# Block products from the first pair on in the second feed-forward of a one-layer encoder step

## The chip, the cores and the metric

The kernel runs on one core of a Trainium2 chip. The metric is the device time of one execution, in microseconds, as the median of several runs. Beside the times there is the trace of one profiled execution, which gives each engine's instructions with their start and length. The engines are TensorE (matmuls; PE in the rows, and PEld for its weight loads), VectorE (DVE), ScalarE (ACT), GpSimd (POOL, which issues the accumulating DMAs) and SyncE (SP, which issues the weight loads).

## The reference

One layer of a streaming encoder over 512 prompt rows and 64 sample rows, 576 in all, width 1024:

```python
x = x + 0.5 * swiglu_ffn(rms_norm(x, ffn1_norm), ffn1_w_gate_up, ffn1_w_down)
h = rms_norm(x, mix_norm); p = h @ w_in        # gated convolutions, merged and multiplied by w_out
...
x = x + merged @ w_out
x = x + 0.5 * swiglu_ffn(rms_norm(x, ffn2_norm), ffn2_w_gate_up, ffn2_w_down)
y = rms_norm(x, final_norm)

def swiglu_ffn(x, w_gate_up, w_down):          # hidden width 2816
    gate, up = jnp.split(x @ w_gate_up, 2, axis=-1)
    return (jax.nn.silu(gate) * up) @ w_down
```

The inputs are float32, and the kernel keeps nearly that precision.

## The kernel before, in words

Activations lie with the feature on the 128 partitions and the 576 rows along the free axis, so x is eight tiles X[0..7] of 128x576. A product of float32 values is made of three matmuls in a shorter type: each operand is split into a high part (rounded) and a low part (the value less its high part), and high x high, high x low and low x high are added in PSUM. A matmul takes 128 features by 288 rows, one half of the rows.

**Plain and block form.** The hidden columns of a feed-forward are worked off in 22 tiles of 128, each with a gate and an up weight; a tile with both is called a pair here. In the plain form (`plain`, line 750) gate and up are two products of 8 feature tiles x 2 halves x 3 matmuls, 96 in all. In the block form (`pair`, line 787) the 2x2 problem of (gate, up) by (first 512 features, last 512 features) and the two halves of the rows is done with seven products in place of eight, in Strassen's way: 7 x 4 feature tiles x 3 matmuls, 84 in all. Its weights are a11, a12 (gate), a21, a22 (up) and four sums s1 to s4 of them; its right operands are parts of the scaled rows themselves for three of the products (a11, a12 and s4), and for four products the "forms" t1 to t4, sums and differences of quarters of the rows, which class `Forms` (line 572) makes: `scale` on ScalarE, `combine` with four VectorE operations and two roundings on ScalarE, `split` with the two low parts on VectorE. `PLAIN` (line 52) says how many pairs are plain: four in the first feed-forward, one in the second.

**Weights.** Class `Stream` (line 195) brings all weights in the order of use, in units of up to 512 features x 128 columns. A raw weight is loaded by an SP queue DMA. `add` makes a weight sum on VectorE, `begin` rounds the unit's high part on ScalarE, and the low part comes in one of two ways. With "dve", VectorE subtracts the high part (`end`). With "dma", ScalarE also writes the negated high part and a POOL DMA adds the raw value onto it. `lead` (line 287) does these ahead of use: when TensorE's code gets unit n, units up to n + 5 are ended, up to n + 7 added and up to n + 6 begun. A unit's two parts live in a pair of tiles of the pool "u" or of another pool, in turn.

**Order.** The calls of each engine are kept in the order of the Python program (class `Ordered`, line 71), so an operation waits for all that the program puts on its engine before it, also where that waits for another engine.

**Around the change.** The products with w_out (loop at line 1132) run j in the order 0, 4, 1, 5, 2, 6, 3, 7. After each, VectorE adds it to X[j], `split_scaled` makes the high (ScalarE) and low part (VectorE) of the row tile times its norm gain, ScalarE squares X[j] for the norm's sum, and the forms are begun. After the loop `gather` adds up the squares and splits the sum, and the last forms are made. Then the second feed-forward begins with plain pair 0, whose gate product takes the feature tiles in the same order, so that X[7] comes last. Between its gate and its up product four matmuls total the squares over the partitions, and `rstd` (line 556) takes the reciprocal root R on VectorE and ScalarE; the gate is multiplied by R before SiLU. Block results stand in one PSUM bank each, eight in all (`bank`, line 157).

Of the kernel before, what the change touches and what calls it, by code (L numbers as in the profile page):

```python
# [13 lines left out]
P = 128  # L14
D = 1024
KT = D // P
# [4 lines left out]
KU = KT // 2  # L21
# [27 lines left out]
WARM = 10  # L49


PLAIN = {"f1": 4, "f2": 1}

IN_TURN = (0, 4, 1, 5, 2, 6, 3, 7)

# [51 lines left out]
def tile_encoder_step(  # L107
# [38 lines left out]
    def wtile(dt=F32, n=LB - HB):  # L146
        return conv.tile([P, LB - HB], dt, tag="w", name=nm("w"), bufs=6)[:, :n]

    def ttile(dt=F32):
        return tmp.tile([P, T], dt, tag="tmp", name=nm("tmp"))  # L150
# [40 lines left out]
    def par(j, r, n=1):  # L191
        return gains[:, r : r + n, j] if r < R_CA else prm[:, r - R_CA : r - R_CA + n, j]
# [115 lines left out]
    def home(other):  # L308

        homes[0] += 1  # L310
        return ("u", other)[homes[0] % 2]
# [13 lines left out]
    def plan_pair(f, gu, i):  # L325

        plan_block((f, "s", i), [
            ws.raw(gu, h * KU * P, KU, gu_col(part, i)) for part in "ug" for h in range(2)  # L330
        ], [home("g") for _ in range(7)], "dve" if (f, i) == ("f1", PLAIN[f]) else "dma")

    def plan_block(name, raws, homes, low="dma"):

        a21, a22, a11, a12 = raws
        s1, s2, s3, s4 = ((name, n) for n in range(1, 5))
        plan[name] = [
            ws.unit(src, KU, home, how, sums)
            for home, (src, how, sums) in zip(homes, (
                (a11, low, ((s1, (a21, a22)),)),  # L340
                (s2, "dve", ((s2, (s1, a11)),)),
                (s1, "dve", ()),
                (s3, "dve", ((s3, (a11, a21)),)),
                (a12, low, ()),
                (s4, "dve", ((s4, (s2, a12)),)),
                (a22, low, ()),
            ))
        ]

    def plan_ffn(f, gu, dn):  # L350
# [24 lines left out]
    def plan_mixer(name, w, col):  # L375
        plan_tile(name, w, 0, (KU, KU), col, "act")
# [12 lines left out]
    for j in range(KT):  # L389
        plan_mixer(("yb", j), w_b_out, j * P)  # L390
    for j in IN_TURN:
        plan_mixer(("o", j), w_out, j * P)
    plan_ffn("f2", ffn2_gu, ffn2_dn)


# [13 lines left out]
    def chunks(name):  # L409

        got = []
        for n in plan[name]:
            w = ws.get(n)
            got += [(w, kk) for kk in range(ws.units[n][1])]
        return got

    def block(w, xs):

        q = bank()[:, :H]
        for k in range(KU):  # L420
            (whi, wlo), (xh, xl) = w, xs[k]
            for m, (l, r) in enumerate(((whi, xh), (whi, xl), (wlo, xh))):
                pe.matmul(q, l[:, k, :], r, start=k == m == 0, stop=k == KU - 1 and m == 2)
        return q
# [19 lines left out]
    def product(name, xs, then=None, order=None, got=None):  # L444

        if name in early:
            return early.pop(name)[:, :, :H]
        ps = psum2()
        if order or got:
            got = got or chunks(name)  # L450
            for n, k in enumerate(order or range(len(xs))):
                mm(ps, *got[k], xs[k], n == 0, n == len(xs) - 1)
        else:
            k = 0
            for n in plan[name]:
                w = ws.get(n)
                for kk in range(ws.units[n][1]):
                    mm(ps, w, kk, xs[k], k == 0, k == len(xs) - 1)
                    k += 1
        take()  # L460
        if then is None:
            dve.time = max(dve.time, pe.time)
            return ps[:, :, :H]
        fill()
        behind.append((pe.time, lambda: then(ps[:, :, :H])))
# [106 lines left out]
    class Forms:  # L572
# [3 lines left out]
        def __init__(self, r_g):  # L576
            self.r_g, self.b, self.t, self.parts = r_g, {}, {}, {}

        def scale(self, p):
            self.b[p] = [wtile(n=T) for _ in range(2)]  # L580
            for b, j in zip(self.b[p], (p, p + KU)):
                sca.activation(b, X[j], AF.Copy, scale=par(j, self.r_g))

        def combine(self, p):
            (b1, b2), (c, d) = self.b.pop(p), (ttile() for _ in range(2))
# [157 lines left out]

    def ffn(f, xg, sums, finish, forms, R=None, todo=()):
        todo = list(todo)

        rest = []


        def plain(i, hs):  # L750
            nonlocal R
            t, up = ttile(), (f, "u", i)
            ps = product((f, "g", i), xg, order=IN_TURN if f == "f2" and i == 0 else None)
            got = None if up in early else chunks(up)
            if R is None:
                R = rstd(sums)
            ups = product(up, xg, got=got)
            hs.append(None)
            at = len(hs) - 1

            def gate():
                dve.tensor_tensor(halves(t), ps, halves(R), op=ALU.mult)
                sca.activation(t, t, AF.Silu)

            def hidden():
                dve.tensor_tensor(halves(t), ups, halves(t), op=ALU.mult)
                hs[at] = high(t)

            def parts():
                hs[at] = hs[at], low(t, hs[at])  # L770

            if f == "f2":
                rest.extend((gate, hidden, parts))
                return
            gate()
            forming()
            hidden()
            forming()
            parts()
            forming()  # L780

        def forming():
            if todo:
                for step, p in todo.pop(0):
                    step(p)

        def pair(i, hs, last):
            qu, uu, t, cu = (ttile() for _ in range(4))
            q1, u2, u3, u4 = half(qu, 0), half(qu, 1), half(uu, 0), half(uu, 1)
            q = []  # L790

            def q7():
                dve.tensor_tensor(u3, q[3], u2, op=ALU.add)
                dve.tensor_tensor(half(cu, 1), u3, q[2], op=ALU.subtract)

            def gate():
                dve.tensor_tensor(half(t, 1), q[5], u4, op=ALU.add)
                dve.tensor_tensor(t, t, R, op=ALU.mult)
                sca.activation(t, t, AF.Silu)

            steps = (
                lambda: sca.copy(q1, q[0]),
                lambda: dve.tensor_tensor(u2, q[1], q1, op=ALU.subtract),
                lambda: dve.tensor_tensor(u4, q[2], u2, op=ALU.subtract),
                q7,
                lambda: dve.tensor_tensor(half(t, 0), q[4], q1, op=ALU.add),
                gate,
            )
            for n, xs in enumerate(bs):
                q.append(block(ws.get(plan[f, "s", i][n]), xs))  # L810
                if n > 0:
                    steps[n - 1]()
                if rest:
                    rest.pop(0)()

            hs.append(None)
            at = len(hs) - 1

            def up():
                if last:  # L820
                    dve.tensor_tensor(t, t, R, op=ALU.mult)
                dve.tensor_tensor(half(cu, 0), q[6], u3, op=ALU.add)

            def hidden():
                dve.tensor_tensor(cu, cu, t, op=ALU.mult)
                hs[at] = high(cu)

            def parts():
                hs[at] = hs[at], low(cu, hs[at])

            rest.extend((up, hidden, parts))

        for g, grp in enumerate(GROUPS):
            hs = []
            for i in grp:
                if i < PLAIN[f]:
                    plain(i, hs)
                    continue
                if i == PLAIN[f]:
                    ws.ahead = AHEAD_UNITS  # L840
                    bs = forms.operands(xg)
                pair(i, hs, grp[-1] == FT - 1)
            while rest:
                rest.pop(0)()
            spare.clear()
            if grp[-1] < FT - 1:
                for j, ps in enumerate(both([(f, "d", g, j) for j in range(2)], hs)):
                    update(j, ps, R)
                for j in range(2, KT):
                    update(j, product((f, "d", g, j), hs), R)  # L850
            else:
                finish(g, hs)
# [279 lines left out]
    for n, j in enumerate(IN_TURN):  # L1132
        ps = product(("o", j), MS)
        dve.tensor_tensor(halves(X[j]), ps, halves(X[j]), op=ALU.add)
        xg[j] = split_scaled(X[j], par(j, R_N2))
        ss.square(X[j])
        ss.add(dve)
        p = n // 2
        if n % 2:
            forms.scale(p)  # L1140
        elif p > 0:
            forms.combine(p - 1)
            if p > 1:
                forms.split(p - 2)
    ss.gather()
    forms.combine(KU - 1)
    forms.split(KU - 2)
    forms.split(KU - 1)


    def finish2(g, hs):
# [112 lines left out]
```

## Time and profile before

| | us |
|---|---|
| median of 3 runs | 1298.48 |
| lowest, highest | 1298.05, 1299.4 |
| the profiled execution's own time | 1297.62 |
| its span, first to last instruction | 1295.8 |

The span is what the rows below are timed in; 1.82 us of the profiled execution lie outside it. TensorE's busy share says little by itself, since matmuls overlap; what counts is whether one group of matmuls starts when the former one's spacing ends. The row of a group gives its start, its length, the engine, the operation, out<-in by names, shapes, the count and, in brackets, the idle time before it with what ended it.

### The profile page before, as it was taken

The page shows a single profiled execution, that of the slowest core. Times are in us where ns is not written, and L with a number is a line of the kernel's source. Part 1 is how long each engine was busy: PE and PEld are TensorE (multiplying, and loading weights), DVE is VectorE, ACT ScalarE, POOL GpSimd, SP SyncE. Part 2 cuts the span into 40 slices and gives each one's busy share as a digit, 9 for nine tenths or more (in the row PEclk, how much of TensorE's full clock was granted, in tenths as well). Part 3 has the DMA queues.
Part 4 walks back from the last instruction along what each step waited for, and adds up shares of the span by engine and source line. Part 5 has one row for each costly group of instructions (what it writes and reads, how often), then busy time and mean ns, then how long its engine had stood idle before and what let it go on. Part 6 is the DMA issues. An engine that isn't in the chain of part 4 may idle for free.

```text
span 1295.8 us, 25664 instructions
## 1 busy us (share of the span) xinstructions
PE 1283.5 (99%) x9754; PEld 1281.9 (99%) x9754; DVE 897.0 (69%) x1480; ACT 763.7 (59%) x1351; POOL 372.0 (29%) x470
## 2 busy tenths in 40 slices
PE   9999999999999999999999999999999999999996
PEld 9999999999999999999999999999999999999996
DVE  6868668648846998898884160336867858847955
ACT  7655646546776655555544674467665656654664
POOL 0032332232333444333321322222242242241230
PEclk9999999999999999999999999999999999999998
DMA  7286786886798898877885977776697696796782
GB/s 215 74 180 153 164 179 153 175 181 151 151 194 185 168 206 175 169 168 169 178 170 117 211 158 164 169 154 139 145 179 171 145 199 149 161 206 140 159 176 80
DMA packets 285931, 213.15 MB, mean 164 GB/s; under 512 B 15344, under 2 KB 248816, under 8 KB 285808
## 3 DMA queue, kind: packets, MB, share of 16 engines
q0 software_dynamic: 57600, 95.05, 44.9%
q1 hardware_dynamic: 226336, 115.49, 31.4%
q8 instruction: 77, 1.26, 0.4%
q10 hardware_dynamic: 1872, 0.97, 0.3%
q14 instruction: 46, 0.38, 0.1%
HBM read 113.81 MB, written 2.62 MB: 90 GB/s over the span
## 4 chain that ended last, share of the span: by engine, by line
PE 96%; DVE 2%; ACT 1%; DMA 1%; issue 0%; DVEq 0%; SPq 0%; ACTq 0%
PE mm L83 96%; DVE acc L83 0%; DMA raw<-in_ffn_w_gate_up_dram 0%; ACT tmp L83 0%; DVE tmp L83 0%; DVE g L83 0%; DVE act L83 0%; DMA gains<-in_params_dram 0%; ACT act L83 0%; DVE x L83 0%; ACT g L83 0%; DVEq L1254 0%; DVE r L83 0%; ACT r L83 0%; ACT acc L83 0%
## 5 line engine op out<-in xcount | busy, mean ns | idle before, releaser
L83 PE MATMUL mm<-act,u 128*128 128x288 f32 x4686 | 659.8, 293 | 0.0
L83 PEld LDWEIGHTS mm<-act,u 128*128 128x128 f32 x4686 | 630.5, 188 | 0.0
L83 PE MATMUL mm<-act,g 128*128 128x288 f32 x2778 | 398.8, 294 | 0.1
L83 PEld LDWEIGHTS mm<-act,g 128*128 128x128 f32 x2778 | 377.5, 188 | 0.3 <-DVE tmp L83 0.3
L83 PE MATMUL mm<-act,act 128*128 128x288 f32 (+2 forms) x2244 | 306.1, 293 | 0.0
L83 PEld LDWEIGHTS mm<-act,act 128*128 128x128 f32 x2244 | 297.3, 188 | 0.0
L83 POOL DMA_DIRECT2D u<-raw x197 | 172.5, 876 | 409.9 <-ACT u L83 298.2
L83 ACT CAST u<-raw 128x512 fp32r<-128x512 f32 (+2 forms) x203 | 116.2, 572 | 156.1 <-PE mm L83 119.1
L83 POOL DMA_DIRECT2D g<-raw x117 | 102.3, 874 | 272.9 <-ACT g L83 212.7
L83 DVE SCALAR_TENSOR_TENSOR w<-g,prm,w 128x606 f32<-128x606 f32 x232 | 179.2, 842 | 1.4 <-ACT w L83 1.4
L83 DVE TENSOR_TENSOR tmp<-mm,tmp 128x288 f32<-128x288 f32 (+1 forms) x239 | 107.6, 458 | 67.8 <-PE mm L83 50.9
L83 POOL DMA_DIRECT2D act<-raw x86 | 74.7, 869 | 196.1 <-ACT act L83 187.7
L83 ACT ACTIVATE u<-u 128x512 fp32r<-128x512 f32 (+2 forms) x197 | 116.9, 593 | 6.2
L83 ACT CAST g<-raw 128x512 fp32r<-128x512 f32 (+2 forms) x126 | 69.0, 548 | 39.1 <-DMA raw<-in_ffn_w_down_dram 15.8
L83 DVE SCALAR_TENSOR_TENSOR tmp<-mm,r 128x576 f32<-128x576 f32 x48 | 36.3, 757 | 71.8 <-PE mm L83 71.8
L83 ACT CAST u<-w 128x512 fp32r<-128x512 f32 x79 | 48.9, 619 | 60.1 <-DVE w L83 52.8
L83 ACT CAST g<-w 128x512 fp32r<-128x512 f32 x77 | 47.7, 619 | 60.1 <-DVE w L83 51.5
L83 ACT CAST act<-tmp 128x576 fp32r<-128x576 f32 x84 | 56.7, 675 | 42.7 <-DVE tmp L83 41.1
L83 DVE TENSOR_TENSOR act<-tmp,act 128x576 fp32r<-128x576 f32 x84 | 62.1, 755 | 18.2 <-ACT act L83 16.5
L83 ACT ACTIVATE g<-g 128x512 fp32r<-128x512 f32 (+2 forms) x117 | 66.4, 568 | 3.7
L83 ACT CAST act<-raw 128x512 fp32r<-128x512 f32 (+3 forms) x94 | 55.6, 592 | 14.5 <-PE mm L83 6.6
L83 DVE TENSOR_TENSOR w<-raw,raw 128x512 f32<-128x512 f32 x78 | 53.4, 685 | 12.8 <-DMA raw<-in_ffn_w_gate_up_dram 12.8
(88 smaller groups left out, 808.6 us busy)
## 6 DMA issues: line engine op xcount, KB each, us to landing
raw<-in_ffn_w_gate_up_dram SPq DMA_DIRECT2D x171, 256.0 KB, 3.4
u<-raw POOLq DMA_DIRECT2D x140, 256.0 KB, 4.1
raw<-in_w_in_dram SPq DMA_DIRECT2D x112, 256.0 KB, 3.6
act<-raw POOLq DMA_DIRECT2D x80, 256.0 KB, 4.0
raw<-in_ffn_w_down_dram SPq DMA_DIRECT2D x96, 192.0 KB, 3.8
g<-raw POOLq DMA_DIRECT2D x60, 256.0 KB, 3.9
g<-raw POOLq DMA_DIRECT2D x43, 192.0 KB, 4.5
u<-raw POOLq DMA_DIRECT2D x41, 192.0 KB, 4.5
```

Source lines behind the costliest of these rows:

```text
L83: return self.tc.keep_in_program_order(fn(*args, **kwargs))
```

## The change

In the second feed-forward pair 0 is done in block form as well (`PLAIN["f2"]` is 0). It runs its seven products in another order, `FORMS_LAST`: a11, a12 and s4, whose right operands are the rows themselves, come first, then the four that need forms. The sums are made in the order that this asks for, its s3 only just before its unit. The sum over squares is totalled, and R taken, after the sixth product, and pair 0's gate is put off into pair 1. For pairs 0 and 1 the low parts of the sums s1 to s4 are made by ScalarE and a POOL DMA in place of VectorE. In the loop over w_out, one scaled copy for the forms follows each X[j], ahead of its square, where two followed every second one behind it; the forms' low parts come earlier; and the gathering of the squares comes behind the last forms and not ahead of them. The weights of these products live in "u" and "g" (the pool of the convolution) in turn, and not in "u" and "act".

```diff
-PLAIN = {"f1": 4, "f2": 1}
+PLAIN = {"f1": 4, "f2": 0}
+
+FORMS_LAST = (0, 4, 5, 1, 2, 3, 6)
...
+            "dma" if f == "f2" and i < 2 else "dve", order_of(f, i))
+
+    def order_of(f, i):
+        return FORMS_LAST if (f, i) == ("f2", 0) else range(7)
+
+    def plan_block(name, raws, homes, low="dma", low_s="dve", order=range(7)):
         a21, a22, a11, a12 = raws
         s1, s2, s3, s4 = ((name, n) for n in range(1, 5))
+        units = (
+            (a11, low), (s2, low_s), (s1, low_s), (s3, low_s), (a12, low), (s4, low_s), (a22, low)
+        )
+        at = (0, 4, 3, 5) if order == FORMS_LAST else (0, 1, 3, 5)
+        sums = dict(zip(at, (
+            (s1, (a21, a22)), (s2, (s1, a11)), (s3, (a11, a21)), (s4, (s2, a12))
+        )))
...
     for j in IN_TURN:
-        plan_mixer(("o", j), w_out, j * P)
+        plan_tile(("o", j), w_out, 0, (KU, KU), j * P, "g")
...
+            order = order_of(f, i)
+            late = ()
+            if order == FORMS_LAST:
+                steps[5], late = (lambda: None), (gate,)
+            q = [None] * 7
+            for m, n in enumerate(order):
+                q[n] = block(ws.get(plan[f, "s", i][m]), bs[n])
+                if R is None and m == 5:
+                    R = rstd(sums)
+                if m > 0:
+                    steps[order[m - 1]]()
                 if rest:
                     rest.pop(0)()
...
-            rest.extend((up, hidden, parts))
+            rest.extend((*late, up, hidden, parts))
...
         xg[j] = split_scaled(X[j], par(j, R_N2))
+        p = n // 2
+        forms.scale(p, (j,))
         ss.square(X[j])
-        ss.add(dve)
-        p = n // 2
-        if n % 2:
-            forms.scale(p)
-        elif p > 0:
+        if n < KT - 1:
+            ss.add(dve)
+        if n % 2 == 0 and p > 0:
             forms.combine(p - 1)
-            if p > 1:
-                forms.split(p - 2)
+        if n in (3, 5, 6):
+            forms.split((n - 2) // 2)
+
+    forms.combine(KU - 1)
+    forms.split(KU - 1)
+    ss.add(dve)
     ss.gather()
-    forms.combine(KU - 1)
-    forms.split(KU - 2)
-    forms.split(KU - 1)
```

## Rows read from the trace of the kernel before

**Rows 1.** The page: busy time of the engines, and the chain's shares.

```profile
PE 1283.5 (99%) x9754; PEld 1281.9 (99%) x9754; DVE 897.0 (69%) x1480; ACT 763.7 (59%) x1351; POOL 372.0 (29%) x470
...
PE 96%; DVE 2%; ACT 1%; DMA 1%; issue 0%; DVEq 0%; SPq 0%; ACTq 0%
```

**Rows 2.** Timeline of TensorE, 897 to 922 us: start, length, engine, operation, count.

```profile
897.66 0.94 PE L83 MATMUL mm<-act,g 128*128 128x288 f32 x6
...
903.90 0.69 PE L83 MATMUL mm<-tmp,ones_r 128*128 128x288 f32 x4
...
910.75 1.74 PE L83 MATMUL mm<-act,g 128*128 128x288 f32 x12
...
921.87 1.74 PE L83 MATMUL mm<-act,u 128*128 128x288 f32 x12
```

**Rows 3.** Stretches: length, busy PE, PEld, DVE, ACT, POOL; clock, DMA share, GB/s.

```profile
1282.00:1286.00 4.00, 2.33 (x16) 1.69 (x14) 3.01 (x7) 2.23 (x6) 0.00 (x0) 1.00 0.69 234
897.60:908.70 11.10, 11.10 (x87) 11.10 (x86) 9.23 (x17) 6.48 (x11) 0.86 (x1) 1.00 0.30 71
```

**Rows 4.** Timeline of ScalarE, 888 to 927 us.

```profile
888.05 1.43 ACT L83 ACTIVATE w<-x,gains 128x576 f32<-128x576 f32 x2
...
892.41 0.78 ACT L83 ACTIVATE act<-x,gains 128x576 fp32r<-128x576 f32 x1 [0.58 <-DVE x L83]
893.09 0.67 ACT L83 ACTIVATE tmp<-x 128x576 f32<-128x576 f32 x1
...
901.54 0.66 ACT L83 CAST tmp<-acc 128x576 fp32r<-128x576 f32 x1
903.95 1.41 ACT L83 CAST act<-tmp 128x576 fp32r<-128x576 f32 x2 [1.74 <-DVE tmp L83]
905.26 0.62 ACT L83 CAST g<-w 128x512 fp32r<-128x512 f32 x1
...
911.22 0.69 ACT L83 ACTIVATE r<-tmp 128x576 f32<-128x576 f32 x1
...
925.48 0.69 ACT L83 ACTIVATE tmp<-tmp 128x576 f32<-128x576 f32 x1 [0.85 <-DVE tmp L83]
926.08 0.60 ACT L83 CAST u<-raw 128x512 fp32r<-128x512 f32 x1
926.71 0.63 ACT L83 ACTIVATE u<-u 128x512 fp32r<-128x512 f32 x1
```

**Rows 5.** Timeline of VectorE, 893 to 926 us.

```profile
893.22 0.82 DVE L83 SCALAR_TENSOR_TENSOR act<-x,gains,act 128x576 fp32r<-128x576 f32 x1 [0.85 <-ACT act L83]
893.96 0.75 DVE L83 TENSOR_TENSOR acc<-acc,tmp 128x576 f32<-128x576 f32 x1
894.63 0.45 DVE L83 TENSOR_TENSOR tmp<-w 128x288 f32<-128x288 f32 x1
...
896.23 1.42 DVE L83 TENSOR_TENSOR act<-tmp,act 128x576 fp32r<-128x576 f32 x2
897.56 0.68 DVE L83 TENSOR_TENSOR w<-w,raw 128x512 f32<-128x512 f32 x1
...
913.52 0.76 DVE L83 SCALAR_TENSOR_TENSOR r<-tmp,r 128x576 f32<-128x576 f32 x1
...
923.84 0.81 DVE L83 TENSOR_TENSOR tmp<-mm,tmp 128x288 f32<-128x288 f32 x2
924.69 0.76 DVE L83 TENSOR_TENSOR tmp<-tmp,r 128x576 f32<-128x576 f32 x1
```

**Rows 6.** Timeline of POOL, 927 to 929 us.

```profile
927.63 0.86 POOL L83 DMA_DIRECT2D u<-raw  x1 [3.69 <-DVE w L83]
```

**Rows 7.** DMA issues at 892.1, 913.4 and 918.3 us: count, KB, us to landing.

```profile
u<-raw POOLq DMA_DIRECT2D x1, 256.0 KB, 6.0
...
g<-raw POOLq DMA_DIRECT2D x1, 256.0 KB, 3.7
...
u<-raw POOLq DMA_DIRECT2D x1, 256.0 KB, 3.2
```

More of the change, by code (lines that the diff above doesn't have):

```diff
@@ L330, in plan_pair @@
             ws.raw(gu, h * KU * P, KU, gu_col(part, i)) for part in "ug" for h in range(2)
-        ], [home("g") for _ in range(7)], "dve" if (f, i) == ("f1", PLAIN[f]) else "dma")
-    def plan_block(name, raws, homes, low="dma"):
+        ], [home("g") for _ in range(7)], "dve" if (f, i) == ("f1", PLAIN[f]) else "dma",
+            "dma" if f == "f2" and i < 2 else "dve", order_of(f, i))
+    def order_of(f, i):
+        return FORMS_LAST if (f, i) == ("f2", 0) else range(7)
+    def plan_block(name, raws, homes, low="dma", low_s="dve", order=range(7)):
         a21, a22, a11, a12 = raws
         s1, s2, s3, s4 = ((name, n) for n in range(1, 5))
-        plan[name] = [
[L338 to L347, printed above, removed]
+        units = (
[5 more added lines that the diff above has]
+        )))
+        plan[name] = [
+            ws.unit(units[n][0], KU, home, units[n][1], (sums[n],) if n in sums else ())
+            for n, home in zip(order, homes)
         ]
@@ L577, in __init__, with scale @@
             self.r_g, self.b, self.t, self.parts = r_g, {}, {}, {}
-        def scale(self, p):
-            self.b[p] = [wtile(n=T) for _ in range(2)]
-            for b, j in zip(self.b[p], (p, p + KU)):
+        def scale(self, p, js=None):
+            for j in js or (p, p + KU):
+                b = wtile(n=T)
                 sca.activation(b, X[j], AF.Copy, scale=par(j, self.r_g))
+                self.b.setdefault(p, []).append(b)
         def combine(self, p):
@@ L750, in plain @@
         def plain(i, hs):
-            nonlocal R
             t, up = ttile(), (f, "u", i)
[L753 to L757, printed above, removed]
+            ps = product((f, "g", i), xg)
+            ups = product(up, xg)
             hs.append(None)
@@ L770, in parts @@
                 hs[at] = hs[at], low(t, hs[at])
-            if f == "f2":
-                rest.extend((gate, hidden, parts))
-                return
             gate()
@@ L787, in pair @@
         def pair(i, hs, last):
+            nonlocal R
             qu, uu, t, cu = (ttile() for _ in range(4))
             q1, u2, u3, u4 = half(qu, 0), half(qu, 1), half(uu, 0), half(uu, 1)
-            q = []
             def q7():
@@ L799, in gate @@
                 sca.activation(t, t, AF.Silu)
-            steps = (
+            steps = [
                 lambda: sca.copy(q1, q[0]),
@@ L807, in pair @@
                 gate,
[L808 to L812, printed above, removed]
+            ]
+            order = order_of(f, i)
[9 more added lines that the diff above has]
+                    steps[order[m - 1]]()
                 if rest:
```

## The prediction

> **What bounds the kernel now.** I read the page first: TensorE is busy for 99% of the span, and the chain that ended last is TensorE for 96% of it [rows 1]. So an edit pays only by what it does to the train of matmuls: fewer of them, or a gap in it. Then I read the timeline of TensorE around the start of the second feed-forward [rows 2]. Pair 0, in plain form, starts at 897.66, its 48 gate matmuls end at 903.90 (6.24 us, 0.130 each), four matmuls of the row sums follow (0.52), and pair 1, the first in block form, starts at 910.75. The reader is to see that one group begins where the former one's spacing ends: TensorE never waits here. Third, the table of stretches [rows 3]: in pair 0's 11.1 us the other engines have room (ScalarE 6.48, the DMA engines 0.30 of their time). Last, the timelines of ScalarE and VectorE, for the order in which each works off its queue; that order decides this case.
>
> **The gain.** A plain pair is 2 x 8 x 6 = 96 matmuls, a block pair 7 x 12 = 84. Plain pair 0 takes 910.75 - 897.66 - 0.52 = 12.57 us; pair 1 in blocks takes 921.87 - 910.75 = 11.12, or 1.59 a block [rows 2]. The change turns one pair from the one into the other: 12.57 - 11.12 = 1.45 us saved if TensorE still never waits. Nothing else is taken off TensorE.
>
> **What moves onto the queues.** The low parts of eight weight sums (four in each of pairs 0 and 1) leave VectorE: per sum one 128x512 subtraction, about 0.68 like the addition at 897.56 [rows 5], gives way to a multiplication on ScalarE, 0.63, and a POOL DMA that lands 3.2 to 3.7 us after its issue [rows 4, 6, 7]. VectorE has no use for the relief, since it didn't hold TensorE; ScalarE gets 8 x 0.63 = 5 us more, within 22 us. Both engines keep the program's order. The trace shows it: the next weight's rounding at 905.26 comes only after the last forms' rounding, issued at 903.95 [rows 4], though its data lay ready.
>
> I number the weight units in the order of use: 0 to 6 pair 0, 7 to 13 pair 1, 14 the first of pair 2. The stream starts unit n + 6 when it gets unit n, so units 0 to 5 are queued before the last output product's own work, and unit 6 only after that product's scaling, the last forms and the gathering of the row sums. Before the change that was harmless: pair 1's units had 12.57 us of plain matmuls ahead of them. Now block 6 is wanted 6 x 1.59 + 0.52 = 10.1 us after the start.
>
> **ScalarE's and VectorE's path, step by step,** from the next to last output product, whose scaled row is there as before, at 892.41 + 0.78 [rows 4]:
> - The new order puts one scaled copy (half of 1.43) before the square that took 893.09 to 893.76. The addition to the row sums starts 0.5 late, at 894.5 in place of 893.96, and the four combinations (1.60 from the first to what follows) end near 896.8 [rows 4, 5].
> - The forms' second rounding (half of 1.41) 897.5, its low part (half of 1.42) 898.25, and sum s3, which now stands here (0.68), 898.9.
> - ScalarE's rounding and negation of s3 (0.60 + 0.63) end at 900.15, and only then comes the last row's scaled rounding (0.78), 900.95; VectorE's low part of it (0.82) ends at 901.8.
> **First wait:** the second block, a12, reaches that row in its fourth quarter at 897.66 + 1.59 + 10 x 0.13 = 900.55. It waits 1.25 us.
> - The last forms: combinations 1.60, 903.4; rounding 0.70, 904.1; low part 0.71, 904.8. Forms-using blocks start after 903.7 and want the last row later still: no wait.
> - Gathering: addition 0.75, 905.55; rounding 0.66, 906.2 [rows 4, 5].
> - Unit 6, rounding and negation: 907.4. POOL issues 0.3 after the negation (927.63 against 926.71 + 0.63), at 907.7 [rows 4, 6]; landing after 3.45 us, the middle of rows 7's 3.2 and 3.7: 911.2.
> **Second wait:** without any wait block 6 would want these low parts in its third matmul, at 897.66 + 10.06 + 0.26 = 907.98. They are 3.2 us late, the first wait included.
> - Units 6 to 11 go through ScalarE at 1.17 each (1.23 less the overlap of 0.06), with one 128x288 copy between them, about 0.3: from 906.2 to 913.5. The root of the row sums stands behind them. In the trace, from ScalarE's part at 911.22 to VectorE's last at 913.52 + 0.76 is 3.06 [rows 4, 5]; here 916.6. Before it was done at 914.28.
> - Four short VectorE operations at 0.40 (two took 0.81), one weight sum at 0.6, the product with the root 0.76: 919.6. SiLU (0.69) 920.3. Behind SiLU on ScalarE stands unit 14: 1.23, 921.5; POOL 921.8; landing 925.3 [rows 4 to 7].
> **Third wait:** without waits block 14 would want it at 897.66 + 14 x 1.59 + 0.52 + 0.26 = 920.7. It is 4.6 us late, the first two waits included, since TensorE cannot pass block 6 or block 14.
>
> **Sum:** -1.45 + 4.6 = +3.15, say +3.2 us. Later units have time again: from pair 2 on only three lows in seven are DMAs, and the gate returns to its own pair.
>
> **The other edits,** at nothing. Output weights in the conv pool in place of the activations': the convolution's tiles there are free long before; if one weren't, a unit would begin a block late, 0 to 1.6 us, and with six units ahead I take 0. A later release of the second gate bank: TensorE's tenth block wants a bank at about 917 to 918, when VectorE is at the release; 0 to 1 us, inside the third wait. Weight loads on SP keep their number. TensorE's clock: the waits are 1.25, 2 and 1.4 us, in separate places; in 1282 to 1286 TensorE was busy 2.33 of 4.00 us and the clock was still 1.00 [rows 3], so I charge nothing.
>
> **The landing time** is the term least sure. Rows 7 show 3.2 and 3.7 where the engines were little used, and 6.0 for a low part that ran with another and a weight load (issued at 892.1). The Trainium skill says in "DMA: Bandwidth & Descriptors", Issuing engines are not separate DMA queues, that DMAs of all issuers run on the same 16 engines and interleave. That speaks against this change, which adds eight to a stretch with loads; the 6.0 agrees with it. By the quiet rows the sum is +3.2; with 6.0 at unit 14 it is +3.2 + 2.5 = +5.7. I take the quiet rows, as VectorE and ScalarE space the last of these issues apart; the ends of this term are +2.9 (3.2) and +5.7.
>
> **Rivals.**
> 1. The queues keep up and only the matmuls count: -1.45 us, 1297.0, faster by less than can be told, not slower. For it: the stretch has much idle ScalarE and DMA time [rows 3]. Against it: the order of the queue, not its load. It decides if unit 6's negation is through by 904.2 (907.98 - 3.45 - 0.3) and unit 14's by 916.9.
> 2. Only block 6 waits, and the SiLU comes early enough to hide unit 14: -1.45 + 3.2 = +1.75, 1300.2, no change that can be told. It decides if the root's ScalarE part runs by 912.1 (913.5 less the 1.4 between 4.6 and 3.2), before the last weights of pair 1 and not behind them. The code says behind.
> 3. DMAs pile up: eight lows within ten us, with loads between them, land at 6.0 in place of 3.45: +5.7, 1304.2. For it: rows 7's 6.0. Against: DMA engines idle for 0.70 of pair 0 before [rows 3].
> 4. A gain above the count: VectorE's relief closes gaps in TensorE's train. There are none in rows 2, so under 5%.
>
> **How the numbers follow.** The profiled execution took 1297.62 us, 1.82 beside its span of 1295.8; the median of three is 1298.48. The sum is made against the profile and carried to the median: 1298.48 + 3.2 = 1301.7. Changes under 0.2% (2.6 us) can't be told from none. Chances: forecast 0.50 (its own range 1300.5 to 1303.5; 0.06 of it under 2.6), rival 3 0.14, rival 2 0.19, rival 1 0.13, rival 4 0.04. Slower: 0.44 + 0.14 = 0.58. Same: 0.06 + 0.19 + 0.13 = 0.38. Faster: 0.04. The range 1297.6 to 1304.4 reaches to rival 3 and past rival 2, and leaves out most of rival 1.
>
> **What would show it.** After: pair 0 in seven groups of 12 matmuls; TensorE waiting for VectorE's or ScalarE's scaled last row some 2.7 us after the feed-forward's start, then for POOL's DMA at block 6, then at pair 2's first block, which stands 3 us later than 921.87 against the start at 897.66. The root's ScalarE part is behind six units' weights. If pair 2's first block starts at 920.4, rival 1 is right; if block 6 waits and pair 2 doesn't, rival 2. The forecast is wrong if either engine passed these operations in another order, or if waits outside this stretch appear.

## The result, and the profile after

The changed kernel takes 1303.38 us (median of 6 runs, 1303.11 to 1304.84) against 1298.37 (6 runs, 1297.96 to 1299.4) in the same runs: ratio 1.0042, interval 1.0032 to 1.0052, so it is slower by 4.2 to 6.8 us. The prediction said 1301.7, in 1297.6 to 1304.4, and slower with a chance of 0.58. The profiled execution took 1304.21 us, with a span of 1302.4.

On the page of the profile after, TensorE's busy share stays at 99%, while its share of the chain falls from 96% [rows 1] to 82%:

```profile
PE 1285.6 (99%) x9742; PEld 1281.9 (98%) x9742; DVE 901.1 (69%) x1487; ACT 769.5 (59%) x1362; POOL 377.1 (29%) x477
...
PE 82%; issue 10%; DMA 2%; DVE 2%; ACT 2%; POOL 2%; POOLq 0%; DVEq 0%; ACTq 0%; SPq 0%
```

The timeline of TensorE after, from the start of the second feed-forward (start, length, engine, operation, count, idle time before it with what ended it), answers to [rows 2], which had no wait at all:

```profile
898.03 1.74 PE L85 MATMUL mm<-act,g 128*128 128x288 f32 x12
...
901.50 0.40 PE L85 MATMUL mm<-act,u 128*128 128x288 f32 x1 [0.55 <-ACT act L85]
902.36 0.54 PE L85 MATMUL mm<-act,u 128*128 128x288 f32 x2 [0.46 <-DVE act L85]
...
910.09 0.53 PE L85 MATMUL mm<-act,g 128*128 128x288 f32 x2 [0.31 <-DVE tmp L85]
911.76 1.60 PE L85 MATMUL mm<-act,g 128*128 128x288 f32 x10 [1.15 <-DMA g<-raw]
...
913.94 1.58 PE L85 MATMUL mm<-act,u 128*128 128x288 f32 x10 [0.31 <-DMA u<-raw]
...
916.19 1.60 PE L85 MATMUL mm<-act,g 128*128 128x288 f32 x10 [0.41 <-DMA g<-w]
...
920.73 1.58 PE L85 MATMUL mm<-act,g 128*128 128x288 f32 x10 [0.85 <-DMA g<-w]
...
927.95 1.59 PE L85 MATMUL mm<-act,g 128*128 128x288 f32 x10 [0.41 <-DMA g<-raw]
...
938.91 1.74 PE L85 MATMUL mm<-act,u 128*128 128x288 f32 x12
...
1253.51 3.65 PE L85 MATMUL mm<-act,g 128*128 128x288 f32 x26 [0.71 <-DMA g<-raw]
```

How to read it: after a block that waits for nothing the next one starts 1.59 us later. What a block takes beyond that is its loss. It is more than the idle time in brackets, by some 0.16 to 0.37 us for each wait; what makes up the rest is not shown. From the starts of all blocks (not all shown): block 1 (a12, the last row) loses 1.53; block 6 loses 0.47 for its PSUM bank, then 1.52 for its low part; blocks 7 to 11 lose 0.57, 0.68, 0.24, 1.10 and 0.17; block 14 loses 0.67. The sum is 6.95. Less the 1.45 that the matmul count saves, that is 5.5, and so it stands: pair 3 starts 938.91 - 898.03 = 40.88 after pair 0, where it was 35.33. Far behind, near 1253, another 0.9 goes.

ScalarE's timeline after (same columns), against [rows 4]: the order is the predicted one.

```profile
900.69 0.76 ACT L85 ACTIVATE act<-x,gains 128x576 fp32r<-128x576 f32 x1
...
907.46 0.63 ACT L85 ACTIVATE g<-g 128x512 fp32r<-128x512 f32 x1
...
909.17 0.38 ACT L85 COPY tmp<-mm 128x288 f32<-128x288 f32 x1
...
914.15 0.67 ACT L85 ACTIVATE r<-tmp 128x576 f32<-128x576 f32 x1
...
920.22 0.68 ACT L85 ACTIVATE tmp<-tmp 128x576 f32<-128x576 f32 x1 [1.75 <-DVE tmp L85]
...
921.44 0.63 ACT L85 ACTIVATE g<-g 128x512 fp32r<-128x512 f32 x1
```

The DMA issues of units 6, 11 and 14 after (issued at 908.38, 914.54 and 922.37; count, KB, us to landing), where [rows 7] had 3.2 and 3.7:

```profile
g<-raw POOLq DMA_DIRECT2D x1, 256.0 KB, 3.3
...
u<-raw POOLq DMA_DIRECT2D x1, 256.0 KB, 7.9
...
g<-raw POOLq DMA_DIRECT2D x1, 256.0 KB, 5.5
```

And the stretches after (length; busy PE, PEld, DVE, ACT, POOL; clock, DMA share, GB/s), then one of before that [rows 3] don't hold, pair 1's:

```profile
897.60:908.70 11.10, 10.09 (x75) 9.65 (x73) 8.75 (x15) 8.49 (x15) 2.04 (x3) 1.00 0.43 94
...
912.00:925.00 13.00, 11.43 (x79) 10.38 (x79) 8.67 (x16) 10.04 (x17) 5.16 (x6) 1.00 1.06 211
```

```profile
910.75:921.87 11.12, 11.12 (x86) 11.12 (x85) 9.33 (x16) 8.19 (x14) 2.50 (x3) 1.00 0.68 143
```

The DMA engines, used at 0.68 in pair 1 before, are full after (1.06, where the highest share read in any stretch of these traces is 1.20), and the clock stays at 1.00.

Not every loss in the list counts by itself. The chain that ended last (start, length, what) doesn't run through pair 1's waits, but through ScalarE's units, the root and SiLU to the landing of unit 14, after which TensorE goes on at 927.95:

```profile
922.37 5.54 DMA g<-raw
```

ScalarE and VectorE wait for no matmul on that way (909 to 922.4), so unit 14 would have landed at 927.9 without the waits of blocks 7 to 11 as well. Block 14 would then have waited for it some 2.8 us longer.

### The profile page after: what moved, and what is told of

Its sections match the earlier page's. It is cut to its first block, busy times and chain, and to the rows that moved or that the text cites. A ratio compares the mean times of both kernels' runs of the same rounds, so it can differ in the third digit from the quotient of the medians.

```text
span 1302.4 us, 25686 instructions
## 1 busy us (share of the span) xinstructions
PE 1285.6 (99%) x9742; PEld 1281.9 (98%) x9742; DVE 901.1 (69%) x1487; ACT 769.5 (59%) x1362; POOL 377.1 (29%) x477
## 4 chain that ended last, share of the span: by engine, by line
PE 82%; issue 10%; DMA 2%; DVE 2%; ACT 2%; POOL 2%; POOLq 0%; DVEq 0%; ACTq 0%; SPq 0%
PE mm L85 82%; DMA g<-raw 1%; POOL u L85 1%; POOL g L85 1%; DVE tmp L85 1%; ACT tmp L85 0%; DMA raw<-in_ffn_w_gate_up_dram 0%; ACT u L85 0%; ACT g L85 0%; DVE act L85 0%; DMA raw<-in_ffn_w_down_dram 0%; ACT act L85 0%; DVE x L85 0%; DVE acc L85 0%; DVE g L85 0%
## 5 line engine op out<-in xcount | busy, mean ns | idle before, releaser
L85 PE MATMUL mm<-act,g 128*128 128x288 f32 x2958 | 425.0, 294 | 3.9 <-DMA g<-raw 2.3
L85 PEld LDWEIGHTS mm<-act,g 128*128 128x128 f32 x2958 | 401.7, 188 | 5.5 <-DMA g<-raw 3.0
L85 PE MATMUL mm<-act,act 128*128 128x288 f32 (+2 forms) x2052 | 280.5, 293 | 0.0
L85 PEld LDWEIGHTS mm<-act,act 128*128 128x128 f32 x2052 | 272.6, 188 | 0.0
L85 POOL DMA_DIRECT2D g<-raw x122 | 105.9, 868 | 301.9 <-ACT g L85 246.7
L85 ACT ACTIVATE u<-u 128x512 fp32r<-128x512 f32 (+2 forms) x202 | 120.0, 594 | 6.4
L85 POOL DMA_DIRECT2D act<-raw x78 | 67.6, 867 | 163.7 <-ACT act L85 155.2
L85 ACT CAST g<-raw 128x512 fp32r<-128x512 f32 (+2 forms) x131 | 72.0, 550 | 38.8 <-DMA raw<-in_ffn_w_gate_up_dram 18.8
L85 ACT ACTIVATE g<-g 128x512 fp32r<-128x512 f32 (+2 forms) x127 | 72.7, 573 | 4.0
L85 ACT ACTIVATE tmp<-tmp 128x576 f32<-128x576 f32 x47 | 32.2, 685 | 46.0 <-DVE tmp L85 45.9
```

The lines of the kernel that those rows point to most:

```text
L85: return self.tc.keep_in_program_order(fn(*args, **kwargs))
```

## The experiments

Theories. **Order**: ScalarE and VectorE come to the last row, unit 6 and unit 14 too late, as forecast; put these earlier and the loss goes. **Pile-up**: the eight added accumulating DMAs fill the DMA engines; bring them down and the loss goes. Later a third was added, that VectorE then is too late to empty the PSUM banks. Kernels of one set ran on one chip beside the kernel before (medians 1298.54, 1298.38 and 1298.38). The table gathers all: in the profiled execution, the time from pair 0's start to pair 3's and from there to the final norm's total, each less that of before (35.33 and 352.08), then the timed runs. The first two columns come from one execution each, and its own time can lie away from the median (run 12: 1303.41 against 1301.85), so small differences in them say little.

| kernel | to pair 3 | behind | median | ratio, interval |
|---|---|---|---|---|
| the change | +5.55 | +0.93 | 1303.38 | 1.0042 (1.0032, 1.0052) |
| 1 lows by VectorE | +6.20 | +0.87 | 1305.98 | 1.0060 (1.0047, 1.0073) |
| 2 DMA lows alone | +2.46 | +0.10 | 1300.87 | 1.0019 (1.0009, 1.0030) |
| 3 unit 6 early | +4.21 | +0.38 | 1302.78 | 1.0037 (1.0025, 1.0050) |
| 4 units 6, 14 early | +4.00 | +0.31 | 1302.70 | 1.0038 (1.0025, 1.0050) |
| 5 and pair 1 by VectorE | +3.43 | +1.98 | 1302.68 | 1.0034 (1.0022, 1.0046) |
| 6 last row early | +4.39 | +0.64 | 1303.03 | 1.0034 (1.0022, 1.0047) |
| 7 all of it | +2.54 | +2.47 | 1302.55 | 1.0032 (1.0019, 1.0044) |
| 8 four pairs by DMA | +12.7 in all | | 1309.61 | 1.0082 (1.0069, 1.0096) |
| 9 before, places shifted | +0.01 | +0.17 | 1298.78 | 1.0002 (0.9993, 1.0011) |
| 10 change, places back | +4.81 | +0.88 | 1303.77 | 1.0039 (1.0026, 1.0051) |
| 11 as 7, places back | +2.54 | +2.28 | 1301.79 | 1.0024 (1.0014, 1.0034) |
| 12 as 11, half by DMA | +4.46 | +0.71 | 1301.85 | 1.0027 (1.0016, 1.0039) |

### 1. The sums' low parts back on VectorE

```diff
-            "dma" if f == "f2" and i < 2 else "dve", order_of(f, i))
+            "dve", order_of(f, i))
```

> The changed kernel with the low parts of all weight sums on VectorE again; order and block form stay. Two theories of the 5.0 us. Queue order: a unit is late because its rounding stands behind other work on ScalarE; unit 6 still stands behind the last row's work, the forms and the row sums, so its wait stays, VectorE gets two subtractions ahead of the last row, and only the way to the root and to pair 2 gets shorter by four negations (2.5 us): 1301 to 1303. Pile-up: the eight extra DMAs fill the DMA engines (share 0.95 to 1.15 from 910 to 924 us) and every landing in that stretch takes 5 to 8 us; without them landings are back at 3.5 to 4.5 and most of the loss goes: 1298 to 1300.

By its median slower than the change itself, though the two intervals overlap (1.0047 to 1.0073, 1.0032 to 1.0052); neither theory foresaw that. TensorE's timeline of this kernel:

```profile
903.16 0.40 PE L85 MATMUL mm<-act,u 128*128 128x288 f32 x1 [1.78 <-ACT act L85]
904.01 0.53 PE L85 MATMUL mm<-act,u 128*128 128x288 f32 x2 [0.45 <-DVE act L85]
904.38 2.59 PE L85 MATMUL mm<-act,g 128*128 128x288 f32 x12
906.77 2.49 PE L85 MATMUL mm<-act,u 128*128 128x288 f32 x12
...
920.62 1.81 PE L85 MATMUL mm<-act,g 128*128 128x288 f32 x12 [0.79 <-DVE tmp L85]
```

The last row is 1.2 us later still, as VectorE has the subtractions to do ahead of it, and banks are waited for at 920. And this gap cost clock, which the stretch of this kernel shows:

```profile
905.00:908.00 3.00, 3.00 (x15) 3.00 (x14) 2.80 (x5) 1.39 (x3) 0.00 (x0) 0.50 0.00 0
```

At 0.50, the lower of the two levels (1.2 GHz), two blocks took 2.39 and 2.33 in place of 1.59: 1.5 us. So with pair 0 in blocks VectorE's subtractions do hold TensorE, by the 1.2 us and the banks.

### 2. The DMA lows alone, in the kernel before

`plan_block` gets the `low_s` of the change, and nothing else is changed; pair 0 stays plain:

```diff
+            "dma" if f == "f2" and i < 3 else "dve")
...
-                (s2, "dve", ((s2, (s1, a11)),)),
+                (s2, low_s, ((s2, (s1, a11)),)),
```

(and so for s1, s3 and s4)

> The kernel before, with pair 0 plain, and the low parts of the sums of pairs 1 and 2 by DMA: the same eight extra DMAs, without the block form of pair 0 and without the new order. Queue order: pair 1's units are begun with 12.6 us of plain matmuls ahead of them, so no wait, 1298 to 1299. Pile-up: fourteen DMAs for low parts in 22 us, with eight loads between them, land late by themselves: 1300 to 1302, with TensorE waiting for DMAs in pairs 1 and 2.

Pairs 1 and 2 alone with DMA lows cost 2.3 us, with none of the change's order. One long wait, and DMA engines near full, in this kernel's TensorE timeline and stretches (before: 0.66 and 0.74 in the same two):

```profile
924.41 1.58 PE L83 MATMUL mm<-act,u 128*128 128x288 f32 x10 [1.18 <-DMA u<-raw]
```

```profile
909.00:920.00 11.00, 11.00 (x85) 11.00 (x84) 7.01 (x11) 9.14 (x16) 4.13 (x6) 1.00 0.95 192
920.00:932.00 12.00, 10.75 (x78) 10.07 (x77) 9.45 (x18) 10.55 (x20) 6.39 (x8) 1.00 0.98 201
```

The unit waited for was issued at 919.52 and took 4.9; at 3.45 it would have come in time (922.97, wanted at 923.07). The pile-up exists by itself.

### 3 and 4. Unit 6 early; units 6 and 14 early

```diff
+    ws.begin()
     forms.combine(KU - 1)
```

and in run 4 besides

```diff
-                steps[5], late = (lambda: None), (gate,)
+                steps[5], late = (lambda: None), (lambda: (ws.begin(), gate()),)
```

> The changed kernel with one call more: unit 6 is begun ahead of the last forms, in place of behind the gathering of the row sums. Queue order: the wait of block 6 (1.15 us for the DMA) goes, forms come about 0.6 us later, and all behind unit 6 on ScalarE comes 1.2 us earlier, the root and pair 2's first unit too: 1.2 to 2 us less than the changed kernel, 1301.4 to 1302.2. Pile-up: the same DMAs in the same 12 us, so what block 6 gains the blocks 8, 10 and 14 lose again: within 0.5 us of the changed kernel, 1303 to 1303.5.

> As the former, and pair 2's first unit is begun ahead of pair 0's SiLU, in place of behind it. Queue order: block 14 no longer waits for the root; what is left is the wait for the last row (1 us) and some bank waits: 1299 to 1300.5. Pile-up: that unit's DMA is issued 2.5 us earlier into full DMA engines and lands with the others, 7 us after issue: 1302 to 1303.5.

The wait at block 6 is gone, so the order was its cause. The time hardly follows. TensorE in run 3, then unit 14's issue on POOL and its landing there:

```profile
915.12 1.60 PE L85 MATMUL mm<-act,g 128*128 128x288 f32 x10 [1.50 <-DMA g<-w]
...
918.27 1.58 PE L85 MATMUL mm<-act,u 128*128 128x288 f32 x10 [1.28 <-DMA u<-w]
...
926.05 1.74 PE L85 MATMUL mm<-act,g 128*128 128x288 f32 x12
```

```profile
921.93 0.86 POOL L85 DMA_DIRECT2D g<-raw  x1 [4.05 <-ACT tmp L85]
```

```profile
g<-raw POOLq DMA_DIRECT2D x1, 256.0 KB, 4.0
```

TensorE, now earlier, meets the low parts of units 8 and 9, which land 4.5 and 6.5 us after their issue: most of the gain is handed on two blocks.

The wait at block 14 (926.05) is gone in both runs, also in run 3, which issues unit 14 as late as the change does (24.30 us after pair 0's start, against 24.34). There it landed after 4.0 us in place of 5.5. Runs 8 and 10 issue it at the same time too (24.32); it lands after 4.8, and block 14 loses under 0.1. So with blocks 7 to 11 as late as they are, it was the landing that made block 14 wait, not the order alone.

### 5. Run 4, with pair 1's lows by VectorE

```diff
-            "dma" if f == "f2" and i < 2 else "dve", order_of(f, i))
+            "dma" if f == "f2" and i < 1 else "dve", order_of(f, i))
```

> As the kernel with units 6 and 14 begun early (1302.7 against 1298.5 before), with the low parts of pair 1's four sums on VectorE again; pair 0's, begun during the output products, stay DMAs. Pile-up theory: with four DMAs fewer in the crowded stretch, blocks 7 to 10 don't wait for landings; the wait for the last row (1.5 us) and a bank (0.3) stay: 1299.3 to 1300.5. Rival, VectorE takes the DMA engines' place: three subtractions more stand ahead of its reading of the row sums' total, so a PSUM bank comes free late and block 8 or 10 waits for that: 1301.5 to 1304.

The waits for DMA at blocks 8 and 9 are gone, with a DMA share of 0.63 in 912 to 925, but two others stand there. TensorE:

```profile
914.07 1.84 PE L85 MATMUL mm<-act,g 128*128 128x288 f32 x12 [0.72 <-DVE tmp L85]
...
918.39 1.81 PE L85 MATMUL mm<-act,g 128*128 128x288 f32 x12 [0.91 <-DVE tmp L85]
```

These are for banks, which VectorE reads out too late. Its reading of the row sums' total shows it, in this run and then in the change:

```profile
913.18 0.75 DVE L85 TENSOR_SCALAR tmp<-mm 128x576 f32<-128x576 f32 x1
```

```profile
911.52 0.75 DVE L85 TENSOR_SCALAR tmp<-mm 128x576 f32<-128x576 f32 x1
```

From pair 0's start these are 15.4 and 13.5 us; three subtractions stand ahead of it here, as the rival had said. VectorE's load by itself doesn't tell it: it is busy for 11.67 of the 13 us here, and for 11.89 in the same stretch of the kernel before, which waits for no bank.

### 6. The last row and units 6, 7 early

```diff
+        if n == KT - 1:
+            ws.ahead = AHEAD_UNITS - 1
...
-        forms.scale(p, (j,))
-        ss.square(X[j])
         if n < KT - 1:
+            ss.square(X[j])
+            forms.scale(p, (j,))
             ss.add(dve)
+        else:
+            forms.scale(p, (j,))
+            ss.square(X[j])
...
-        if n in (3, 5, 6):
+        if n in (3, 5):
...
+    ws.begin()
     forms.combine(KU - 1)
+    forms.split(KU - 2)
     forms.split(KU - 1)
+    ws.begin()
+    ws.begin()
```

> The changed kernel (1303.4) with the last row's scaled form freed of what stood ahead of it: square ahead of the scaled copy, the third forms' low parts behind the last row, unit 5 begun behind it; units 6 and 7 are begun before the gathering. If each wait of TensorE is a cost of its own, the last row's 1.5 us and block 6's 1.5 go: 1300.2 to 1301.2. If the DMA engines are the bound from 910 to 924, all that is gained before block 8 is waited for again there: 1302.3 to 1303.

Blocks 1 and 6 wait for neither row nor low part. Most of that is lost again at blocks 8 and 9. TensorE, ScalarE, POOL and a stretch of this kernel:

```profile
912.30 0.42 PE L85 MATMUL mm<-act,g 128*128 128x288 f32 x2
915.80 1.78 PE L85 MATMUL mm<-act,g 128*128 128x288 f32 x10 [3.08 <-DMA g<-w]
917.38 3.08 PE L85 MATMUL mm<-act,u 128*128 128x288 f32 x12
```

```profile
908.63 0.62 ACT L85 CAST g<-w 128x512 fp32r<-128x512 f32 x1 [1.85 <-DVE w L85]
```

```profile
910.21 0.86 POOL L85 DMA_DIRECT2D g<-w  x1 [3.23 <-DVE tmp L85]
```

```profile
917.00:920.00 3.00, 3.00 (x15) 3.00 (x14) 2.90 (x6) 1.25 (x3) 0.50 (x1) 0.51 1.11 193
```

Unit 8's low part was issued at 910.21 and took 5.5. With the 3.45 of the forecast it would have landed at 913.7, and block 8, which wants it at 912.56, would have waited 1.1: of the 3.1 some 2.0 are the crowded DMA engines, 1.1 the order (ScalarE waited for VectorE's sum, which stood behind the gathering). The gap was followed by 3.4 us at the lower clock, and block 9 took 2.88: 1.3 of the loss is clock.

### 7. All of 4, 5 and 6 together

The edit joins the diffs of 5 and 6 and the second diff of 4.

> The former two together: last row, units 5 to 7 and 14 early, pair 1's low parts of sums on VectorE. If queue order and the pile-up are the whole loss, TensorE hardly waits: 1297 to 1299, at or under the kernel before. If VectorE becomes the bound (late reading of the total, bank waits): 1300 to 1303.

The last row, the low parts of blocks 6 to 14 and the clock are all in order, and the kernel still takes 1302.55. The two waits for banks stand as in run 5 (1.10 and 0.89), and four losses of some 0.6 us for DMA (0.31 to 0.47 idle) come at the start of groups' down projections and just before them (934, 960, 1048 and 1251). So the VectorE theory holds here, and order and pile-up together are not the whole loss.

### 8. Four pairs by DMA

```diff
-            "dma" if f == "f2" and i < 2 else "dve", order_of(f, i))
+            "dma" if f == "f2" and i < 4 else "dve", order_of(f, i))
```

> The changed kernel with the low parts of the sums by DMA in four pairs in place of two: the suspected cost doubled, in pairs that stand clear of the start. Pile-up: seven accumulating DMAs and four loads a pair want more DMA time (some 13.8 us by their mean shares) than a pair has (11.1), so each of the two further pairs costs 2 to 2.7 us: 1307 to 1309, DMA share 1.0 or more in pairs 2 and 3. If the loss is only the order at the start: 1303 to 1304.

With twice the DMA lows the kernel takes 6.2 us more than the change, with new waits in pair 2 and at pair 4's first block (955.58). TensorE, ScalarE and a stretch of this kernel:

```profile
931.84 1.58 PE L85 MATMUL mm<-act,g 128*128 128x288 f32 x10 [1.09 <-DMA g<-w]
...
955.58 1.59 PE L85 MATMUL mm<-act,g 128*128 128x288 f32 x10 [2.74 <-DMA g<-raw]
```

```profile
950.68 0.62 ACT L85 CAST g<-raw 128x512 fp32r<-128x512 f32 x1 [8.36 <-DMA raw<-in_ffn_w_gate_up_dram]
```

```profile
931.00:942.00 11.00, 9.83 (x72) 9.58 (x72) 6.64 (x12) 9.43 (x18) 6.04 (x7) 1.00 1.13 219
```

The full share goes on as long as the DMA lows do, up to 948 us: the pile-up grows with them. It reaches the weight loads too: those issued from 938 to 942 landed after some 12 us, and ScalarE waited 8.36 us for one of them before it could begin the unit that pair 4 then waited for.

### 9 to 11. The places of the later units

Pair 0 has seven units now, not four, so all later units change places between the pools "u" and "g". That might explain the late waits. The same edit in the kernel before (9), in the change (10) and in run 7 (11):

```diff
                 if i >= PLAIN[f]:
+                    if (f, i) == ("f2", 1):
+                        homes[0] += 1
                     plan_pair(f, gu, i)
```

> The kernel before with one edit: from pair 1 of the second feed-forward on, all weight units change places between the pools u and g, as they do in the changed kernel, where pair 0 has seven units in place of four. Theory (the places cause the late waits): TensorE waits 0.3 to 0.8 us for DMA at the beginning of down projections, near 954, 1042 and 1247, as in the changed kernels; +0.6 to +2.0 us, 1299 to 1300.4. Rival (the late waits come from loads that stand later behind the crowded start, or from TensorE being ahead of them): no such waits, 0 us, 1298.1 to 1298.7.

> The changed kernel, its units from pair 1 on put back into the places that they have in the kernel before. Theory (places): the wait at 1251 to 1253 goes (0.9 us), nothing else changes, so 1302.4 to 1302.6; up to pair 3's start still +5.5. At the border of pairs 0 and 1 two units in a row share a pool, which may cost a wait at blocks 6 to 8. Rival (places don't matter): 1303.1 to 1303.7, the late wait stays.

> The kernel with the last row early, units 6 and 14 early and pair 1's low parts by VectorE, its units from pair 1 on put back into the places of the kernel before. It had lost 2.5 us up to pair 3's start and some 2 in four waits at down projections behind it. Theory (places): the four late waits go, 1300.2 to 1301.0. Rival (places don't matter): 1302.3 to 1302.9.

The theory falls: run 9 has no such wait and the time of before, and runs 10 and 11 keep theirs, in the other pool. TensorE in run 10, then in run 11:

```profile
1252.07 3.70 PE L85 MATMUL mm<-act,u 128*128 128x288 f32 x26 [0.50 <-DMA u<-raw]
```

```profile
1251.51 3.64 PE L85 MATMUL mm<-act,u 128*128 128x288 f32 x26 [0.74 <-DMA u<-raw]
```

Run 11 also keeps the two waits for banks (1.09 and 0.90). It has the lowest median of all variants with pair 0 in blocks, 1301.79, but its interval overlaps run 7's, and it is slower than before.

### 12. Half of pair 1's lows by DMA

Run 11 with `i < 2` again, and for pair 1 alone s1 and s4 by VectorE:

```diff
+        low_1 = "dve" if name == ("f2", "s", 1) else low_s
...
-            (a11, low), (s2, low_s), (s1, low_s), (s3, low_s), (a12, low), (s4, low_s), (a22, low)
+            (a11, low), (s2, low_s), (s1, low_1), (s3, low_s), (a12, low), (s4, low_1), (a22, low)
```

> As the run before, but two of pair 1's four sums (s2, s3) have their low parts by DMA and two (s1, s4) by VectorE. If the waits for banks (1.10 and 0.89 us) shrink with VectorE's load faster than the DMA engines fill, TensorE loses about 1 us at the start in place of 2.5: 1299 to 1300.5. If the DMA engines fill first: waits for DMA at blocks 8 and 9 in their place, no better than the run before.

The DMA engines fill first. TensorE of this kernel:

```profile
913.37 0.50 PE L85 MATMUL mm<-act,u 128*128 128x288 f32 x2 [0.46 <-DVE tmp L85]
916.33 1.72 PE L85 MATMUL mm<-act,u 128*128 128x288 f32 x10 [2.46 <-DMA u<-w]
```

The next block took 2.88 at the lower clock. No variant with pair 0 in blocks beats the kernel before.

## Why the prediction was right, and where its size was off

The forecast was 1301.7, slower by 3.2 us; measured is 1303.38, slower by 5.0. The path that it gave is the one that the trace shows; one term of it was too small.

- **The gain**, 1.45 from the count: nothing contradicts it. The page counts 12 matmuls fewer (9742 against the 9754 of [rows 1]). Pair 2, without a wait after block 14's, goes at the old pace.
- **ScalarE's and VectorE's path**: right, step by step. Pair 0 starts 0.37 later in this trace; with that added, forecast and measured are 901.3 and 901.45 for the last row's rounding, 908.1 and 908.38 for unit 6's issue, 913.9 and 914.15 for the root, 922.2 and 922.37 for unit 14's issue.
- **First wait**: 1.25 forecast, 1.53 measured, for the two releasers named (0.55 for ScalarE, 0.46 for VectorE). **Second wait**: 3.2 with the first, measured 3.52, and unit 6 landed after 3.3. Its own part is 1.99, of which 0.47 was not foreseen in kind: block 6 first waits for a bank, because ScalarE's copy of block 0's result (909.17) stands behind units 6 and 7. Run 6 confirms both by taking them away, run 3 the second.
- **The landing time** is the step that failed: "I take the quiet rows, as VectorE and ScalarE space the last of these issues apart". They don't space them enough. POOL issued units 8 to 13 in 1.17 to 1.74 us each, and landings rose from 3.3 to 7.9 at a DMA share of 1.06; unit 14, issued as forecast, took 5.5 in place of 3.45. SP's weight loads came later too: those issued from 910 to 920 us landed after 6.3 at the median, after 3.5 in that stretch before. The Trainium skill ("DMA: Bandwidth & Descriptors", Issuing engines are not separate DMA queues) says that all issuers' DMAs interleave on the same engines. The prediction weighed that, and this trace agrees with it.
- **What that step cost.** Blocks 7 to 11 lost 2.76 us that the forecast had at nothing; at 3.45 each the first of them would have landed before its third matmul (909.55 + 3.45 = 913.0 against 913.5), and so would the next. Unit 14 landed at 922.37 + 5.5 = 927.9; at 3.45 it would have been 925.8. An estimate from these rows: with 3.45 throughout, block 14 wants its unit at 924.6 and waits 1.2, so all waits together are 4.7, where the forecast had 4.6. With 5.5 at unit 14 alone they are 6.8. With the landings of units 7 to 11 alone they are 6.3, which is what run 10 shows (4.81 + 1.45). Measured are 6.95, so either would have made most of the loss.
- **The quiet rows** were not quiet: the DMA share was 0.71 and 0.74 while the low parts with 3.7 and 3.2 were under way, and 0.66 for the one with 6.0. Below a full share the rows don't say what sets the landing time.
- **Third wait**: 1.4 forecast at block 14 (4.6 less 3.2), 0.67 measured, but not for the reason that the sum gave: with blocks 7 to 11 as late as they were, a landing after 3.45 would have been in time (925.8 against 927.4). Its mechanism (root, SiLU, unit 14) is the chain that ended last. In run 1, where that unit landed after 3.3, block 14 still waited for it (0.89).
- **Rival 3**, the pile-up, had the better sum (1304.2, at a chance of 0.14) and was on top of the forecast, not in its place. It priced unit 14's landing at 6.0, which took 5.5; that pair 1's blocks would wait too it did not say. **Rivals 1 and 2** fall by their own conditions: unit 6's negation ended at 908.1 (needed: 904.2), the root's ScalarE part began at 914.15 (needed: 912.1).
- **"VectorE has no use for the relief"** was wrong: in run 1, without it, the last row comes 1.2 us later and banks are waited for. **The second gate bank** and the pools, at nothing, cost nothing visible in the change itself. **The clock**, at nothing, was right for the waits that came (1.00 throughout), but only for these: runs 1, 6 and 12 lost 1.3 to 1.5 us to it.
- **Outside the stretch**: the forecast called itself wrong if waits appear outside this stretch, and there is one, 0.9 near 1253. By that sign it failed.

Why does removing any one wait pay so little? At the start of this feed-forward several chains reach TensorE at nearly the same time: the landings on full DMA engines (1.06 with eight DMA lows in pairs 0 and 1), the order on ScalarE, and VectorE's order once the lows of pair 1 are back on it (run 5). The plain pair had been the cover: 12.57 us that want neither forms nor new sums [rows 2, 3], for 1.45 us of matmuls. That they hand the loss to each other is shown (runs 3 to 7 and 12); that no other arrangement could hold all three off is not.

Two things stay open. The late waits: ScalarE's timeline of the change shows a load that came late,

```profile
1250.40 0.52 ACT L85 CAST u<-raw 128x384 fp32r<-128x384 f32 x1 [1.54 <-DMA raw<-in_ffn_w_down_dram]
```

and the DMA engines are at 1.13 to 1.16 there; but they are at 1.10 to 1.15 in the same stretch of before, without a wait. It has no slack in either; what tips it is not settled, only that the places don't (9, 10). And from pair 0's start to the end the two traces differ by 6.5 us where the medians differ by 5.0, so the waits may be shorter in other executions. Landing times differ between traces as well (unit 14: 5.5, and 4.8 in runs 8 and 10, issued alike).

## What to carry to other kernels

Before replacing covered work by faster work, work out for each resource (each engine's queue order, the DMA engines, the banks) what load it gets per microsecond of the new, shorter stretch, and not only when each single step is done: the steps on ScalarE and VectorE were forecast to within 0.5 us here, and the sum missed the one shared resource. Price a moved DMA by the rows of a stretch as full as the new one will be, not by quiet rows. When taking away a wait hands most of it to the next one, follow the chain that ended last, and count the waits that stand behind it before taking away another.

## What the runs showed of the hardware that was not expected

- A 256 KB accumulating DMA landed after 3.3 us as the first of a row of such DMAs (issued at 908.38) and after 7.9 us as the sixth (914.54), at a DMA share of 1.06; pairs 1 and 2 with four more of them each raised the share from 0.66 and 0.74 to 0.95 and 0.98 (run 2). A 256 KB weight load issued by SP landed after 3.5 us at the median from 910 to 920 before, after 6.3 in the change, and after some 12 in run 8 (938 to 942, share 1.13).
- The clock after a gap: waits of 1.78 and 0.45 us close together (run 1), 3.08 (run 6) and 2.46 after one of 0.46 (run 12) were each followed by some 3.5 us at the lower level, in which a block took 2.3 to 2.9 us in place of 1.59. A gap of 2.74 after one of 0.50 in run 8 left it at 1.00. So the length of a gap alone did not tell.
